# Two heads' score matmuls, and their products with values, issued as one run of four; rotary keys padded with zero rows

## Chip, cores and metric

The kernel runs on one core of one Trainium2 chip. The metric is the device time of one execution in microseconds (us); lower is better. TensorE (PE in the profile) multiplies matrices, with its weight loads shown as PEld; VectorE (DVE), ScalarE (ACT) and GpSimd (POOL) do the elementwise work, and SyncE (SP) issues the transfers.

## The reference

Four layers over 256 tokens of width 1024, batch 1, all in float32. What matters here are the attention parts:

- Layer 1 (AB): 8 heads of block attention with ALiBi ("moba", which at 256 tokens is plain causal attention) and 8 heads of forgetting attention ("fox"). Head width 64.
- Layer 2 (CD): 4 heads of differential attention (two score maps of width 64 each, values of width 128), and 8 heads of sliding-window attention ("swa") of width 64, where four query heads share one key head.
- Layer 3: latent attention ("MLA") with 8 heads; the score of a head is a product over 128 plain features plus a product over 64 rotary features, and the rotary keys are the same for all heads.
- Layer 4: stick-breaking attention. After layers 3 and 4 follow cross-attention to a memory and an MLP of width 4096.

```python
# one causal head of fox; moba, diff and swa have the same shape of work
s = einsum('bhqd,bhsd->bhqs', q, k) * scale + bias      # scores
p = softmax(where(causal, s, -inf))
o = einsum('bhqs,bhsd->bhqd', p, v)                     # product with values
# MLA: q = [q_nope (128) | q_rope (64)], k = [k_nope (128) | k_rope (64), shared by the heads]
```

## The kernel before

**Tiles.** The 256 queries and keys are two tiles of 128. Scores of a head are two matmuls in float32 into one PSUM bank: queries 0 to 127 against keys 0 to 127 (128 columns), and queries 128 to 255 against all 256 keys. Two heads of width 64 lie above each other in one transposed tile `qT[j]`, `kT[j]` (partitions 0 to 63 and 64 to 127), so a score matmul works on 64 of TensorE's 128 rows. In the profile these are the matmuls of form `64*128`. The product with values of moba, fox and swa has 64 columns of values as its weights, so it fills 64 of the 128 columns of the array (form `128*64`); two heads go to the two halves of the partitions of one bank. In MLA the rotary part of a score is again a matmul on 64 rows, added into the same bank as the plain part on 128 rows.

The trace has two matmul instructions for each of these float32 matmuls; they are called passes below. The large projections are not float32 matmuls: weights and activations are split into a high and a low part (type fp32r, form `psum<-r,r`), and three matmuls of one pass each stand for one product.

**Order.** Nothing is issued while the program is described. `Plan` records each instruction with its reads and writes, and `schedule` then simulates the five engines with a cost for each instruction, picks at each step the ready instruction with the longest chain behind it, gives out the slots of SBUF and PSUM, and so fixes an order for every engine. Each engine then runs its queue in that order. An attention part therefore does not run alone: between its matmuls the plan sets projection matmuls of the same or of the next stage.

**Names.** `scores` issues the two matmuls of one head; `soft` adds the bias, takes the maximum and the exponential on DVE and ACT; `normed` divides by the sums; `probs_T` transposes the probabilities with three TensorE transposes and a copy; `pv_feat` issues the two matmuls with the values; `gated` multiplies by the gate. In `layer_ab`, `layer_cd` and `mla` these are called head by head. `pairs_T` makes the transposed tiles, of the rotary keys `kpT` too. PSUM has 8 banks; at most 4 are given out for scores ("S").

Of the kernel before, what the change touches and what calls it, by code (L numbers as in the profile page):

```python
# [15 lines left out]
OP = mybir.AluOpType  # L16
AX = mybir.AxisListType.X
PSUM = bass.MemoryType.PSUM


# ======================================================================
# Recording: views of tiles that have no address yet
# ======================================================================
class Buf:
    """A tile to be: its slot is picked when its first instruction is scheduled."""

    def __init__(self, tag, np_, shape, dtype, name):
        self.tag, self.np_, self.dtype, self.name = tag, np_, dtype, name
        self.row = int(np.prod(shape))
        self.log = []          # (op, writes, p0, p1, mask)  # L30
        self.left = 0          # accesses not scheduled yet
        self.slot = None
        self.free_at = 0.0
        self.first = self.last = None


class Pool:
    """Slots for tiles. use[i]: the slots in use while instruction i runs, if from now on all
    instructions ran in the order of the program; as long as that fits, no deadlock is possible."""
# [114 lines left out]
# how long after the end of an instruction another engine may start  # L154
# [11 lines left out]
class Plan:  # L166
# [7 lines left out]
    # -- tiles  # L174
# [3 lines left out]
    def tag(self, name, pool, most=99, dtype=F32):  # L178
        """A kind of tile that lives in a pool, at most `most` at a time as long as others wait."""
        self.tags[name] = dict(pool=self.pools[pool], psum=pool == "psum", most=most, dtype=dtype, used=0)  # L180
# [11 lines left out]
    # -- instructions  # L192
    def op(self, forms, reads, writes, kind=""):
        """forms: {engine: (ns, call)}: the engines it may run on."""
        o = Op()
# [5 lines left out]
        for v, w in [(v, False) for v in reads] + [(v, True) for v in writes]:  # L201
            b = v.buf
# [12 lines left out]
            for e in b.log:  # L215
# [4 lines left out]
                # an older access that this write hides entirely need not be kept  # L220
# [11 lines left out]
    def either(self, *calls):  # L232
        """One instruction that any of several engines may run: (engine, method, args, kw) each."""
# [9 lines left out]
    # -- scheduling  # L243
    def schedule(self):
# [36 lines left out]
        def can(b):  # L281
            tg = self.tags[b.tag]
            p = tg["pool"]
            if b.first <= front:
                return bool(p.free)
            if not p.free or tg["used"] >= tg["most"]:
                return False
            return p.use[front:b.first].max() < p.bufs
# [11 lines left out]
        while n < len(ops):  # L300
# [23 lines left out]
            if e == "T":  # L324
                # the first by priority that the loading of its operand doesn't delay
# [10 lines left out]
            bad = next((b for b in news if not can(b)), None)  # L336
# [3 lines left out]
            # another engine that would be done with it sooner  # L340
# [71 lines left out]
    # -- emission  # L412
# [34 lines left out]
class _Eng:  # L447
    """Stands for an engine while the instructions are recorded."""
# [23 lines left out]
def make(plan, e, method, args, kw):  # L472
    """((cost, call), reads, writes, act tables) of one instruction."""
# [79 lines left out]
# pools of tiles: elements in a partition, tiles  # L553
POOLS = {"k4": (1024, 5), "k2": (512, 33), "r2": (512, 46), "k1": (256, 18), "k128": (128, 11), "k16": (16, 64),
         "kr": (128, 3), "psum": (512, 8)}
# kinds of tiles: pool, the most at a time
# [8 lines left out]
class Net:  # L565
# [26 lines left out]
    def copy(self, out, in_):  # L592
        """A copy, on ACT or DVE."""
# [6 lines left out]
    def wpiece(self, src, f, pat, fill="", parts=1, **kw):  # L600
        """One piece of a weight matrix, f elements in each partition, as hi and lo in parts of equal size."""
# [15 lines left out]
    def wtiles(self, w, k0, nk, c0, nc_, fill=""):  # L617
        """Weight rows of the chunks k0.., columns c0..: pieces of (hi, lo, first chunk, chunks)."""
# [23 lines left out]
    def new_T(self, n=NC8):  # L642
        """(hi, lo) of a transposed activation: a list over the chunks of [128, 256] views each."""
# [9 lines left out]
    def mm3(self, ps, st, mv, first, last):  # L653
        """ps += st.T mv, both operands as (hi, lo)."""
# [5 lines left out]
    def mm_tok(self, ps, xt, wh, wl, kc, kmap, t, first, last):  # L660
        """ps[tokens of t, :] += X W, the activations stationary."""
# [8 lines left out]
    def proj_tok(self, w, xt, c0, ncol, k0=0, nk=NC8, ps=None, first=True, last=True, x0=0, cls="acc", fill=""):  # L670
        """Both token tiles of X W[:, c0:c0+ncol] in PSUM."""
# [7 lines left out]
    def mm_feat(self, ps, first_in_bank, xt, wh, wl, c, last):  # L679
        """ps[features, 256 tokens] += W.T X.T for a chunk, the weights stationary."""  # L680
# [5 lines left out]
    def proj_feat(self, w, xt, c0, ncol, nk=NC8, cls=("acc", "acc"), fill=""):  # L686
        """W[:, c0:c0+ncol].T X.T: feature blocks of 128, two to a bank."""
# [20 lines left out]
    def rows_T(self, tag, n, parts):  # L708
        """Rows of 128 from DRAM, transposed into columns [128, n]."""
# [88 lines left out]
    def squares(self, x):  # L798
        """Sums of the squares of the rows, [128, tiles]; x[t] has two halves."""
# [14 lines left out]
    def setup_late(self):  # L814
# [22 lines left out]
        nc.vector.tensor_scalar(self.lam, self.lam, LAM_INIT, None, op0=OP.subtract)  # -lambda  # L837
# [31 lines left out]
    def new_x(self):  # L869
        """The residual's transpose: banks of two chunks, [128, 2, 256] each."""  # L870
        return [self.nc.tile([128, 2, 256], "x", "x") for _ in range(4)]

    def stats_sum(self, x):
        """x: [128, k, 256] views; the sums of squares over the features, [128 tokens, tiles] in PSUM."""
# [18 lines left out]
    def stats_x(self, ss=None):  # L893
        """rstd of the residual's rows: [128, tiles]."""
# [11 lines left out]
    def gained(self, x, g0):  # L906
        """x.T times the gain, as hi and lo."""
# [11 lines left out]
    def rstd_bc(self, r):  # L919
        """rstd along the free dimension, the same in every partition: [128, 256]."""  # L920
# [10 lines left out]
    def out_proj(self, w, yt, pieces):  # L931
        """x += (Y W).T for a [*, 1024] matrix; pieces: (first chunk, chunks, half of the columns)."""
# [25 lines left out]
    def qk_scale(self, qk, t):  # L958
        """qk: raw projections of token tile t; the per-head RMS norm without gain, in place."""
# [20 lines left out]
    def pairs_T(self, src, np_, g=None):  # L980
        """src[t] [128 tokens, np_*128]: its transpose, np_ views [128, 256], times a column."""
# [15 lines left out]
    def scores(self, qT, kT, rows):  # L997
        nc = self.nc
        s = self.ps("S")
        nc.tensor.matmul(s[:, 0:128], qT[rows, 0:128], kT[rows, 0:128], start=True, stop=True)  # L1000
        nc.tensor.matmul(s[:, 128:384], qT[rows, 128:256], kT[rows, 0:256], start=True, stop=True)
        return s

    def soft(self, s, b0, b1, sums=None, init=None, scale=None):
        """exp(s + bias - max), or of -scale * (s + bias),
        for the causal blocks (q0 | k0), (q1 | k0 k1); returns it and -max."""
# [12 lines left out]
    def probs_T(self, e):  # L1019
        """[128 q, (q0k0 | q1k0 | q1k1)] -> [128 k, (k0: q0 q1 | k1: q1)]."""  # L1020
# [13 lines left out]
    def gate(self, w, xt, c0, rbc):  # L1034
        """2 silu(g).T of 512 columns: 4 views [128, 256]."""
# [12 lines left out]
    def gated(self, yt, c, p, g, k):  # L1048
        """k * p * g into the chunk c of yt."""
# [4 lines left out]
    def values(self, w, xt, c0, n=512):  # L1054
        """A projection with the tokens on the partitions: a tile for each token tile."""
# [7 lines left out]
    def q_or_k(self, w, xt, c0, g=None):  # L1063
        """A projection of 512 columns, normalised per head and transposed: 4 views [128, 256], two heads each."""
# [7 lines left out]
    def normed(self, e, sums):  # L1072
        """The exponentials of soft over their sums."""
# [3 lines left out]

    def pv_feat(self, o, v, sl, pt):
        """o = (P V).T of a causal head; sl: its columns of v."""
# [5 lines left out]
    def forget(self, w, xt):  # L1085
        """FOX: c = cumsum(log f) in columns, -c in every partition along the keys (two tiles of 4 heads)."""
# [45 lines left out]
    def layer_ab(self):  # L1132
# [5 lines left out]
        for mix in range(2):  # L1138
# [7 lines left out]
            for j in range(4):  # L1146
                op = self.ps("O")[:, :256]
                for s in range(2):
# [541 lines left out]
```

## Time and profile before

| | |
|---|---|
| median of 3 runs | 987.67 us (986.16 to 987.92) |
| span of the profiled execution | 990.0 us |
| own time of the profiled execution beside its span | not given apart from it |
| mean granted TensorE clock | 0.994 of full speed |
| TensorE matmuls busy | 962.9 us, 97% |
| VectorE busy | 680.6 us, 69% |
| ScalarE busy | 571.4 us, 58% |
| transfers | 157.13 MB, mean 159 GB/s |

A busy time of matmuls contains the pipeline behind each one: a matmul of 256 columns is listed with some 280 ns although the next one starts much earlier. So the cost of a matmul is read from the distance between starts, not from its duration. All instructions carry line 533, the helper that emits them; forms, shapes and times tell them apart.

### The profile page before, as it was taken

What the parts mean: (1) busy time and instruction counts of PE and PEld (TensorE: products, weight loads), DVE (VectorE), ACT (ScalarE), POOL (GpSimd) and SP (SyncE); (2) the same over time, 40 slices, a digit from 0 to 9 for tenths busy, and PEclk for the clock granted to TensorE, in tenths of its full rate; (3) what the DMA queues carried; (4) which work ended last, traced back from release to release, by engine and by line L of the source; (5) the groups of instructions that cost most, each with busy time, mean ns of one, the idle gap of its engine ahead of it and who ended that gap; (6) DMA issues with size and microseconds to landing.
All of it is one profiled execution on the core that took longest, in us unless ns stands there. A gap on an engine that the chain in (4) does not pass through costs nothing.

```text
span 990.0 us, 18191 instructions
## 1 busy us (share of the span) xinstructions
PE 962.9 (97%) x6829; PEld 874.0 (88%) x6829; DVE 680.6 (69%) x1561; ACT 571.4 (58%) x1310; POOL 59.9 (6%) x94
## 2 busy tenths in 40 slices
PE   7899999999999999999999999899999999999997
PEld 5577778888979889999999999899899999999985
DVE  7687686787987854896655456765768777556654
ACT  5675585557676675775555445644666754344443
POOL 2124000040210200000000000000000000000000
PEclk9999999999999999999999999999999999999999
DMA  7978424654413523664565456635535554555641
GB/s 193 285 191 207 113 85 150 212 149 131 145 34 90 154 94 115 211 192 141 171 204 180 149 192 203 181 128 165 166 117 168 174 170 144 179 189 176 203 154 43
DMA packets 96678, 157.13 MB, mean 159 GB/s; under 512 B 9831, under 2 KB 28493, under 8 KB 96589
## 3 DMA queue, kind: packets, MB, share of 16 engines
q1 hardware_dynamic: 96236, 154.91, 50.8%
q8 instruction: 53, 0.87, 0.4%
q0 software_dynamic: 352, 1.06, 0.3%
q14 instruction: 37, 0.30, 0.1%
HBM read 154.89 MB, written 1.06 MB: 158 GB/s over the span
## 4 chain that ended last, share of the span: by engine, by line
PE 81%; DMA 9%; DVE 4%; ACT 2%; SPq 1%; issue 1%; POOL 1%; POOLq 0%; DVEq 0%; ACTq 0%
PE psum L533 81%; DMA k<-in_w_in_ab_dram 4%; DVE r L533 2%; DMA k<-in_mlp_w_out_dram 2%; DMA k<-in_sb_w_qkv_dram 2%; ACT r L533 2%; SPq L533 1%; DVE k L533 1%; ACT k L533 1%; POOL k L533 1%; DMA k<-in_mla_w_ukv_dram 0%; DMA k<-in_mla_w_uq_dram 0%; POOLq L1686 0%; DVEq L533 0%; ACTq L533 0%
## 5 line engine op out<-in xcount | busy, mean ns | idle before, releaser
L533 PE MATMUL psum<-r,r 128*128 128x256 f32 (+2 forms) x6018 | 891.9, 305 | 9.8 <-ACT r L533 9.1
L533 PEld LDWEIGHTS psum<-r,r 128*128 128x128 f32 x6018 | 795.6, 190 | 69.1 <-ACT r L533 13.3
L533 DVE TENSOR_TENSOR r<-k,r 128x512 fp32r<-128x512 f32 (+2 forms) x669 | 407.5, 648 | 149.2 <-ACT r L533 73.1
L533 ACT ACTIVATE r<-k 128x512 fp32r<-128x512 f32 (+2 forms) x568 | 310.7, 592 | 203.7 <-PE psum L533 84.2
L533 PE MATMUL psum<-k,k 128*128 128x128 f32 (+8 forms) x771 | 149.0, 316 | 10.3 <-DMA k<-in_x_dram 4.5
L533 ACT ACTIVATE k<-psum 128x256 f32<-128x256 f32 (+4 forms) x168 | 70.5, 451 | 124.0 <-PE psum L533 120.6
L533 PEld LDWEIGHTS psum<-k,k 128*128 128x128 f32 (+3 forms) x771 | 94.9, 166 | 38.3 <-issue 12.1
L533 POOL TENSOR_TENSOR k<-k,k 128x2 f32<-128x2 f32 (+3 forms) x42 | 49.8, 1200 | 884.9 <-DVE k L533 833.5
L533 ACT ACTIVATE k<-k 128x256 f32<-128x256 f32 (+4 forms) x147 | 71.7, 507 | 19.7 <-DVE k L533 15.4
L533 ACT ACTIVATE k<-k,k 128x256 f32<-128x256 f32 (+3 forms) x152 | 64.7, 450 | 19.1 <-DVE k L533 15.9
L533 DVE CAST r<-k 128x512 fp32r<-128x512 f32 (+2 forms) x101 | 40.0, 402 | 28.9 <-PE psum L533 12.2
L533 DVE TENSOR_TENSOR k<-k 128x256 f32<-128x256 f32 (+3 forms) x40 | 13.8, 344 | 40.9 <-ACT k L533 39.6
L533 DVE TENSOR_TENSOR k<-k,k 128x512 f32<-128x512 f32 (+5 forms) x86 | 40.3, 478 | 2.3 <-ACT k L533 1.3
L533 DVE TENSOR_TENSOR k<-psum,k 128x512 f32<-128x512 f32 (+2 forms) x53 | 33.4, 635 | 11.6 <-PE psum L533 11.3
L533 ACT ACTIVATE r<-k,k 128x256 fp32r<-128x256 f32 x64 | 29.7, 500 | 16.2 <-DVE k L533 15.1
L533 DVE SCALAR_TENSOR_TENSOR r<-k,k,r 128x256 fp32r<-128x256 f32 x72 | 34.3, 494 | 2.4 <-ACT r L533 1.5
L533 DVE TENSOR_TENSOR r<-psum,r 128x256 fp32r<-128x256 f32 (+1 forms) x52 | 24.0, 480 | 16.3 <-ACT r L533 14.7
L533 ACT ACTIVATE r<-psum 128x256 fp32r<-128x256 f32 (+1 forms) x49 | 20.7, 435 | 14.1 <-PE psum L533 13.8
L533 DVE TENSOR_SCALAR k<-k,k 128x128 f32<-128x128 f32 (+7 forms) x88 | 21.6, 274 | 5.2 <-POOL k L533 4.7
L533 ACT ACTIVATE k<-psum,k 128x512 f32<-128x512 f32 (+1 forms) x18 | 11.6, 650 | 13.2 <-PE psum L533 13.2
L533 DVE CUSTOM_DVE_ANT_0 k<-psum,k 128x256 f32<-128x256 f32 (+1 forms) x48 | 15.0, 353 | 4.8 <-PE psum L533 4.5
L533 DVE CUSTOM_DVE_ANT_0 k<-psum,k,k 128x256 f32<-128x256 f32 (+1 forms) x32 | 12.1, 414 | 8.3 <-PE psum L533 8.2
(39 smaller groups left out, 165.0 us busy)
## 6 DMA issues: line engine op xcount, KB each, us to landing
k<-in_mlp_w_in_dram SPq DMA_DIRECT2D x64, 512.0 KB, 4.6
k<-in_mlp_w_out_dram SPq DMA_DIRECT2D x64, 512.0 KB, 4.5
k<-in_w_in_ab_dram SPq DMA_DIRECT2D x32, 512.0 KB, 7.0
k<-in_w_in_cd_dram SPq DMA_DIRECT2D x26, 512.0 KB, 4.6
k<-in_sb_w_qkv_dram SPq DMA_DIRECT2D x24, 512.0 KB, 4.7
k<-in_xa_w_kv_dram SPq DMA_DIRECT2D x16, 512.0 KB, 5.5
k<-in_w_out_ab_dram SPq DMA_DIRECT2D x8, 512.0 KB, 3.7
k<-in_w_out_cd_dram SPq DMA_DIRECT2D x8, 512.0 KB, 4.5
```

The lines of the kernel that those rows point to most:

```text
L533: return getattr(eng, method)(*[real(a) for a in args], **{k: real(v) for k, v in kw.items()})
```

## The change

Three edits. First, `scores` takes both heads of a pair, and issues their four matmuls as one planned instruction, in the order: head 0 queries 0 to 127, head 1 queries 0 to 127, head 0 queries 128 to 255, head 1 queries 128 to 255. This holds for moba, fox and swa (pairs of heads) and for the two maps of a differential head. Second, `pv_pair` does the same for the products with values of moba, fox and swa: it is issued when the transposed probabilities of both heads are there. Third, in MLA the rotary keys are kept in two tiles of 128 rows, one with the keys in the upper 64 rows and zeros below, one the other way round, so that the rotary matmuls work on all 128 rows. The plan gets a new call `group` with a cost of its own, and `can` counts several new tiles of one instruction. The diff removes comments as well; these lines are left out here.

```diff
+    def group(self, *calls):
+
+        cost, load, gos, reads, writes = 190.0, None, [], [], []
+        for args, kw in calls:
+            (c, go, ld), r, w, _ = make(self, "T", "matmul", args, kw)
+            cost += 104 + 0.805 * args[2].size
+            load = ld if load is None else load
+            gos.append(go)
+            reads += r
+            writes += w
+
+        def go():
+            for g in gos:
+                g()
+
+        return self.op({"T": (cost, go, load)}, reads, writes, "group")
...
-        def can(b):
+        def can(b, before):
+
             tg = self.tags[b.tag]
             p = tg["pool"]
+            k = sum(self.tags[x.tag]["pool"] is p for x in before)
             if b.first <= front:
-                return bool(p.free)
-            if not p.free or tg["used"] >= tg["most"]:
+                return len(p.free) > k
+            if len(p.free) <= k or tg["used"] + sum(x.tag == b.tag for x in before) >= tg["most"]:
                 return False
-            return p.use[front:b.first].max() < p.bufs
+            return p.use[front:b.first].max() + k < p.bufs
...
-    def scores(self, qT, kT, rows):
-        nc = self.nc
-        s = self.ps("S")
-        nc.tensor.matmul(s[:, 0:128], qT[rows, 0:128], kT[rows, 0:128], start=True, stop=True)
-        nc.tensor.matmul(s[:, 128:384], qT[rows, 128:256], kT[rows, 0:256], start=True, stop=True)
-        return s
+    def scores(self, qT, kT):
+
+        res = [self.ps("S") for _ in range(2)]
+        calls = []
+        for q, k in ((slice(0, 128), slice(0, 128)), (slice(128, 256), slice(0, 256))):
+            for i, s in enumerate(res):
+                rows = slice(64 * i, 64 * i + 64)
+                o = s[:, 0:128] if q.start == 0 else s[:, 128:384]
+                calls.append(((o, qT[rows, q], kT[rows, k]), dict(start=True, stop=True)))
+        self.nc.group(*calls)
+        return res
...
+    def pv_pair(self, o, v, sls, pts):
+
+        calls = []
+        for k, (a, b), c in ((0, (0, 256), 0), (1, (256, 384), 128)):
+            for i, (sl, pt) in enumerate(zip(sls, pts)):
+                calls.append(((o[64 * i:64 * i + 64, c:256], v[k][:, sl], pt[:, a:b]),
+                              dict(start=k == 0, stop=k == 1, skip_group_check=True)))
+        self.nc.group(*calls)
...
             for j in range(4):
-                op = self.ps("O")[:, :256]
-                for s in range(2):
+                pts = []
+                for s, sc in enumerate(self.scores(qT[j], kT[j])):
                     h = 2 * j + s
-                    rows = slice(s * 64, (s + 1) * 64)
-                    sc = self.scores(qT[j], kT[j], rows)
...
                     self.normed(e, sums)
-                    self.pv_feat(op[rows], v, slice(h * 64, (h + 1) * 64), self.probs_T(e))
+                    pts.append(self.probs_T(e))
+                op = self.ps("O")[:, :256]
+                self.pv_pair(op, v, [slice(h * 64, (h + 1) * 64) for h in (2 * j, 2 * j + 1)], pts)
                 self.gated(yt, 4 * mix + j, op, g[j], 0.5)
...
-                for m in range(2):
-                    sc = self.scores(qT[h], kT[h], slice(m * 64, (m + 1) * 64))
+                for m, sc in enumerate(self.scores(qT[h], kT[h])):
...
-        kpT, = self.pairs_T([k.rearrange("p r d -> p (r d)") for k in kpd], 1)
+        p = self.ps("T")
+        for t in range(NT):
+            self.tr(p[:, t * 128:(t + 1) * 128], kpd[t].rearrange("p r d -> p (r d)"))
+
+        kpT = [self.t2([128, 256], "kpT") for _ in range(2)]
+        for s in range(2):
+            nc.gpsimd.memset(kpT[s][64 - 64 * s:128 - 64 * s], 0.0)
+            self.copy(kpT[s][64 * s:64 * s + 64], p[64 * s:64 * s + 64, :256])
...
-                nc.tensor.matmul(sc[:, 0:128], qpT[hh // 2][rows, 0:128], kpT[rows, 0:128], start=False, stop=True)
+                nc.tensor.matmul(sc[:, 0:128], qpT[hh // 2][:, 0:128], kpT[s][:, 0:128], start=False, stop=True)
                 nc.tensor.matmul(sc[:, 128:384], qn[h // 2][:, h % 2, 128:256], kn[h // 2][:, h % 2], start=True, stop=False)
-                nc.tensor.matmul(sc[:, 128:384], qpT[hh // 2][rows, 128:256], kpT[rows], start=False, stop=True)
+                nc.tensor.matmul(sc[:, 128:384], qpT[hh // 2][:, 128:256], kpT[s], start=False, stop=True)
```

In `layer_cd` the loop of swa is changed as the one of `layer_ab`.

## Rows read from the trace of the kernel before

**Rows 1.** The page: busy us, share of the span, instructions.

```profile
PE 962.9 (97%) x6829; PEld 874.0 (88%) x6829; DVE 680.6 (69%) x1561; ACT 571.4 (58%) x1310; POOL 59.9 (6%) x94
```

**Rows 2.** Who TensorE waited for after 85 us: us, times, longest.

```profile
PE psum L533 <- ACT r L533: 5.4, 6, 3.7
...
PE psum L533 <- DVE r L533: 0.2, 1, 0.2
```

**Rows 3.** The chain that ended last, in order of time: start, length, what.

```profile
78.17 5.36 DMA k<-in_w_in_ab_dram
...
85.24 182.24 PE psum L533 x1184
```

**Rows 4.** TensorE matmuls by form: rows*columns of the array, output, count, busy, mean ns.

```profile
L533 PE MATMUL psum<-k,k 64*128 64x256 f32 x80 | 19.8, 429 | 0.0
...
L533 PE MATMUL psum<-k,k 128*64 128x256 f32 x48 | 10.0, 404 | 0.0
```

**Rows 5.** Timeline of TensorE matmuls in fox: start, us from first start to last end.

```profile
119.87 0.40 PE L533 MATMUL psum<-r,r 128*128 128x512 f32 x1
120.20 0.49 PE L533 MATMUL psum<-k,k 64*128 64x128 f32 x4
120.62 0.38 PE L533 MATMUL psum<-r,r 128*128 128x256 f32 x1
120.84 0.40 PE L533 MATMUL psum<-r,r 128*128 128x256 f32 x2
...
121.75 0.70 PE L533 MATMUL psum<-k,k 64*128 64x256 f32 x4
122.38 0.51 PE L533 MATMUL psum<-r,r 128*128 128x256 f32 x2
```

**Rows 6.** Timeline, an unbroken run of projection matmuls in the first MLP.

```profile
604.81 5.46 PE L533 MATMUL psum<-r,r 128*128 128x256 f32 x45
```

**Rows 7.** Timeline, the scores of swa; a row is named by its first form.

```profile
273.27 0.93 PE L533 MATMUL psum<-k,k 64*128 64x128 f32 x8
274.13 0.62 PE L533 MATMUL psum<-r,r 128*128 128x256 f32 x3
...
277.01 0.92 PE L533 MATMUL psum<-k,k 64*128 64x128 f32 x4
277.86 0.97 PE L533 MATMUL psum<-r,r 128*128 128x256 f32 x6
278.76 0.92 PE L533 MATMUL psum<-k,k 64*128 64x128 f32 x4
```

**Rows 8.** Timeline, products with values in fox.

```profile
118.72 0.65 PE L533 MATMUL psum<-k,k 128*64 128x256 f32 x2
119.30 0.97 PE L533 MATMUL psum<-r,r 128*128 128x256 f32 x4
...
134.82 0.65 PE L533 MATMUL psum<-k,k 128*64 128x256 f32 x4
135.40 0.97 PE L533 MATMUL psum<-r,r 128*128 128x256 f32 x4
```

**Rows 9.** Timeline, the first and the last matmuls on half an array.

```profile
78.85 0.49 PE L533 MATMUL psum<-k,k 64*128 64x128 f32 x2
...
372.23 0.70 PE L533 MATMUL psum<-k,k 64*128 64x256 f32 x2
372.85 0.33 PE L533 MATMUL psum<-k,k 128*128 128x128 f32 x1
```

**Rows 10.** Stretch, length; busy PE, PEld, DVE, ACT, POOL; PEclk; DMA share; GB/s.

```profile
75.00:160.00 85.00, 83.80 (x531) 62.99 (x530) 63.90 (x197) 55.21 (x150) 9.64 (x8) 0.98 0.49 137
...
265.00:288.00 23.00, 21.93 (x147) 17.02 (x146) 20.99 (x82) 18.49 (x63) 6.36 (x8) 1.00 0.27 78
288.00:297.00 9.00, 9.00 (x63) 5.94 (x60) 6.08 (x19) 5.58 (x16) 0.00 (x0) 1.00 0.00 0
340.00:375.00 35.00, 35.00 (x226) 28.80 (x224) 22.07 (x72) 26.25 (x71) 0.86 (x1) 1.00 0.33 106
```

More of the change, by code (lines that the diff above doesn't have):

```diff
@@ L335, in schedule @@
             news = [b for b in o.bufs if b.slot is None]
-            bad = next((b for b in news if not can(b)), None)
+            bad = next((b for n_, b in enumerate(news) if not can(b, news[:n_])), None)
             if bad is not None:
@@ L1236, in layer_cd @@
         for j in range(4):
-            op = self.ps("O")[:, :256]
-            for s in range(2):
+            pts = []
+            for s, sc in enumerate(self.scores(qT[j], kT[j // 2])):
                 h = 2 * j + s
-                rows = slice(s * 64, (s + 1) * 64)
-                sc = self.scores(qT[j], kT[h // 4], rows)
                 bw = self.t2([128, 256], "bw")
@@ L1250, in layer_cd @@
                 self.normed(e, sums)
-                self.pv_feat(op[rows], v, slice(h // 4 * 64, (h // 4 + 1) * 64), self.probs_T(e))
+                pts.append(self.probs_T(e))
+            op = self.ps("O")[:, :256]
+            self.pv_pair(op, v, [slice(j // 2 * 64, (j // 2 + 1) * 64)] * 2, pts)
             self.gated(yt, 4 + j, op, g[j], 0.5)
@@ L1373, in mla @@
                 hh = 4 * g + h
-                rows = slice(s * 64, (s + 1) * 64)
                 sc = self.ps("S")
                 nc.tensor.matmul(sc[:, 0:128], qn[h // 2][:, h % 2, 0:128], kn[h // 2][:, h % 2, 0:128], start=True, stop=False)
-                nc.tensor.matmul(sc[:, 0:128], qpT[hh // 2][rows, 0:128], kpT[rows, 0:128], start=False, stop=True)
+                nc.tensor.matmul(sc[:, 0:128], qpT[hh // 2][:, 0:128], kpT[s][:, 0:128], start=False, stop=True)
                 nc.tensor.matmul(sc[:, 128:384], qn[h // 2][:, h % 2, 128:256], kn[h // 2][:, h % 2], start=True, stop=False)
-                nc.tensor.matmul(sc[:, 128:384], qpT[hh // 2][rows, 128:256], kpT[rows], start=False, stop=True)
+                nc.tensor.matmul(sc[:, 128:384], qpT[hh // 2][:, 128:256], kpT[s], start=False, stop=True)
                 sums = self.sm([128, NT], "msum")
```

## Prediction

> **What bounds the kernel now.** I read the page first: TensorE's matmuls are busy for 97% of the span, VectorE for 69%, ScalarE for 58% [rows 1]. Then TensorE's waits: after 85 us it waits for anyone for 8.5 us in all, in ten pieces and by five rows, of which the longest and the shortest are shown [rows 2]. Then the chain that ended last: up to 85 us it runs through weight transfers, after that through TensorE in long pieces, one of them from 85 to 267 us without a break [rows 3]. So from 85 us on a microsecond taken out of TensorE's queue is a microsecond of the kernel, as long as VectorE and ScalarE keep up. Because a busy TensorE need not be an efficient one, the last view is the timeline, from start to start. In an unbroken run of projection matmuls 256 columns take (5.46 - 0.28) / 44 = 0.118 us each [rows 6].
>
> **What a stay on half the array costs.** The matmuls on 64 rows or 64 columns stand in short runs between full-size ones; I call such a run a visit. Take one at 120.20 us [rows 5]. The 512-column matmul ahead of it started at 119.87; 512 columns at the granted 2.4 GHz stream for 0.21 us, so with 0.01 between neighbours the next could have started at 120.09: entering costs 0.10. Start of the visit to start of the next full matmul is 0.42. That next matmul then needs 0.22 to its successor instead of 0.118: another 0.10. So each visit costs 0.20 on top of its own length. That extra is 0.15 where a transpose follows; I use 0.20 throughout.
>
> The lengths, from the visit's start to the next full matmul: two heads, 128 columns: 0.42; two heads, 256 columns: 0.63 [rows 5]; one head, 256 columns: 0.62 [rows 9]; one head with both: 0.85; two heads with both, eight passes: 0.86 [rows 7]; values, 256 columns, one head 0.58 and two heads 0.58 [rows 8]. Taking 0.107 (256 float32 columns need two clocks each, 0.213 per pass; 128 need 0.107) off each of two passes, values with 128 columns come to 0.37, one head's scores with 128 columns to 0.41.
>
> Two things are to be seen. The second head is free when it stands beside the first: eight passes take as long as four. And the plan before already pairs heads often, but not always, and rarely joins the 128- and the 256-column part.
>
> **Counting.** There are 73 visits in the timeline, the first at 78.85, the last at 372.23 us [rows 9]. They hold 160 passes on 64 rows and 96 on 64 columns: 80 and 48 with 256 columns [rows 4], and as many with 128.
>
> - 47 on rows: 10 of one head with 128 columns (4.2 us), 8 with 256 (5.0), 9 of two heads with 128 (3.8), 9 with 256 (5.7), 6 of one head with both (5.1), 3 of two heads with nearly all (2.6), 2 mixed as long as a 256 (1.3): 27.7.
> - 26 on columns: 5 and 7 with 128 (4.4), 5 and 6 with 256 (6.4), 3 longer ones (0.8, 0.8, 1.5): 13.9.
> - 73 x 0.20 for entering and leaving: 14.6.
>
> Before: 56.2 us.
>
> After: 16 score groups (4 moba, 4 fox, 4 diff, 4 swa) at 0.86 + 0.20 = 17.0. Twelve value groups: two heads with 256 columns take 0.58, the two 128-column passes add 0.21 behind them, so 0.79 + 0.20, 11.9. MLA's rotary matmuls leave half-array mode: I let the step from 64 to 128 rows add nothing, since 128-row matmuls also stream a column per clock (256 in 0.118 us [rows 6]), so 8 heads x (2 x 0.107 + 2 x 0.213) = 5.1, and 0.2 for four steps of 0.005 to 0.01 a head. After: 34.2 us. **TensorE gets 22.0 us shorter**: some 10 in layer AB, 1.6 in diff, 5 in swa, 5 in MLA. Bounds: if each visit cost 0.15 instead of 0.20, the 45 visits that go away give 2.2 less; nothing in the rows gives more than 22.
>
> **What costs nothing, and why.** One more copy of 64 x 256 on ScalarE or VectorE and two fills on GpSimd, which is 6% busy [rows 1]. An instruction of ScalarE takes 26.25 / 71 = 0.37 us in MLA's stretch [rows 10]. The three are needed only when MLA's first scores start, after TensorE has projected queries, keys and values; without that cover they would cost three times that, 1.1 us, and nothing in them can gain time. The two tiles take one slot more of the 256-element pool. A score group needs two score banks at once out of four, which the plan enforces; a value group waits for both heads' probabilities, so its first head's product comes later and `gated` with it; behind it in TensorE's queue stand the projection matmuls.
>
> **Where the gain is not paid out.**
> - The first visits (78 to 85 us) lie where the chain runs through a weight transfer [rows 3]: 0.7 us lost.
> - In swa, 265 to 288 us, VectorE is busy for 20.99 of 23.00 us [rows 10]. It can follow TensorE by at most 2.0 us there; score visits shrink by 3.1 (7 visits, 7.4 us, to 4 x 1.06). 1.1 lost. At 288 to 297 VectorE has 2.9 us free for the other 2.0. In AB it has 21 of 85 free, for 10; in MLA ScalarE has 8.7 of 35 free, for 5 [rows 10].
> - All costs and readiness change, so the plan is drawn anew from about 78 us on, and the 8.5 us of waits will fall elsewhere. I add 1.0, an eighth of them, as an estimate; bounds -3 to +5.
>
> Sum against the profiled execution: 990.0 - 22.0 + 0.7 + 1.1 + 1.0 = 970.8. The median of the runs shown is 987.67, 2.3 below that span, so **968.5 us**, 1.9% faster.
>
> **A rule against it.** Eight passes of two heads took 0.86 us and four of one head 0.85 [rows 7], and 0.58 stands against 0.58 for values [rows 8]: passes of different halves ran together in whatever order they were queued. The Trainium skill, "TensorE: Matmul & The Clock Gate", Part 3, "The mechanism", says that matmuls start and end strictly in program order and only weight loads overtake. By that the sum would be 974.5, as worked out for the second rival; the rows here speak against it.
>
> **Rivals.**
> 1. *VectorE becomes the bound in the attention parts.* For: 91% busy in 265 to 288, and 63.90 of 85 in AB [rows 10], which becomes 85% if TensorE takes 75 us. Against: TensorE has projection matmuls to fill with, and the long chain piece covers all of fox. If swa's 5.1 and half of AB's 10 are lost: 968.5 - 1.1 (counted already) + 10.1 = 977.5.
> 2. *Passes overlap only at the seams of calls.* Each float32 call is two passes. If head 1's first pass must wait for head 0's second to start, a score group streams 0.107 + 0.107 + 0.213 + 0.213 + 0.213 = 0.85 instead of 0.64, a value group likewise: 28 x 0.21 = 6.0, giving 974.5. Against: rows 7 and 8.
> 3. *Slower: the value group blocks TensorE's queue.* In swa the heads follow each other by 1.75 us (277.01 to 278.76 [rows 7]), VectorE's pace. If the second head's probabilities are late by that each time and nothing is queued ahead, 12 groups cost 21 us: 989.5. It decides from 1.6 us a group (19.2 / 12); slower by over 0.2% from 1.8. Against: the plan places the group where it believes both are ready, and puts six projection matmuls between two visits even in swa.
> 4. *No change:* the pairs were together already, or another resource sets the pace. Against: 47 + 26 visits for what 28 can hold; the transfers use 0.49 of the DMA engines at most in these stretches [rows 10].
>
> **How the numbers follow.** Forecast 0.64 (own range 962 to 975: all 22.0 paid out and the waits 3 shorter gives 963, the waits 5 longer and 2.2 less gained 975), rival 1 0.20, rival 2 0.06, rival 3 0.06, no change 0.04. What a measurement of this kernel can tell from no change is about 0.2%, 2 us. Faster 0.64 + 0.20 + 0.06 = 0.90, within 0.2% 0.04, slower 0.06. The range reaches from 962 to 980, so that rival 1 is inside and rivals 3 and 4 are left out.
>
> **What would show it.** Passes of form 64*128 fall from 160 to 128, float32 passes on the full array rise by 32; 28 visits instead of 73, of 0.86 and 0.79. Right: TensorE's waits after 85 us stay near 8.5 and layer AB ends some 9 us earlier. Rival 1: waits for VectorE or ScalarE grow by several us between 75 and 300. Rival 2: score groups last 1.07. Rival 3: TensorE waits over a microsecond ahead of 128*64 runs. I am wrong if the new order opens waits outside the attention parts, which no row of before can show.

## The result, and the profile after

The changed kernel takes 970.56 us (median of 4 runs, 969.73 to 971.15); the kernel before, beside it, 987.13 (986.16 to 987.92). The ratio is 0.9825, interval 0.9809 to 0.9842: 16.6 us faster, where 19.2 were forecast, inside the range.

The span went from 990.0 to 968.0, by just the 22.0 us that the forecast takes out of TensorE. That is chance. The executions of the kernel before spread from 984.24 to 990.56 us over 29 runs. A time is some 1.7 us above its span (986.43 for 984.7), so the one profiled took some 991.7, more than any of them; a second profile of it has a span of 984.7 (first experiment below). Against that one the traces differ by 16.7, as the medians do. So the second trace of before stands for it from here on.

The page of the changed kernel, busy time by engine; it answers to [rows 1]:

```profile
span 968.0 us, 18191 instructions
...
PE 940.2 (97%) x6829; PEld 869.6 (90%) x6829; DVE 679.3 (70%) x1565; ACT 573.7 (59%) x1311; POOL 57.9 (6%) x96
```

TensorE has as many matmuls as before and is 22.7 us less busy than in the first profile, 19.4 less than in the second (959.6); all other engines are within 2.3 us of where they were. The forms, as in [rows 4]:

```profile
L552 PE MATMUL psum<-k,k 128*128 128x256 f32 x80 | 23.3, 382 | 0.1
...
L552 PE MATMUL psum<-k,k 64*128 64x256 f32 x64 | 10.6, 380 | 0.0
L552 PE MATMUL psum<-k,k 64*128 64x128 f32 x64 | 9.2, 320 | 1.3 <-DVE k L552 1.2
L552 PE MATMUL psum<-k,k 128*64 128x256 f32 x48 | 7.8, 402 | 0.0
L552 PE MATMUL psum<-k,k 128*64 128x128 f32 x48 | 4.7, 273 | 0.0
```

Passes on 64 rows fell from 160 to 128, as forecast. In the timeline they make 15 visits, those on 64 columns 11: 26, because two score groups (at 98.48) and two value groups (at 279.45) stand back to back, where 28 were forecast and 73 stood before.

Timeline of TensorE in fox, changed kernel: start, length, form of the first matmul of a run, count. It answers to [rows 5, 7, 8]:

```profile
123.45 0.93 PE L552 MATMUL psum<-k,k 64*128 64x128 f32 x8
124.30 0.98 PE L552 MATMUL psum<-r,r 128*128 128x256 f32 x6
...
127.65 0.87 PE L552 MATMUL psum<-k,k 128*64 128x256 f32 x8
128.45 0.50 PE L552 MATMUL psum<-r,r 128*128 128x512 f32 x1
```

A score group lasts 124.30 - 123.45 = 0.85 us (0.86 forecast), a value group 0.80 (0.79). Eleven of the sixteen score groups are like that; four before 104 us and one in swa are longer, by 1.3 us together (below, at the wait for the second bank). Who TensorE waited for after 85 us, answering to [rows 2]:

```profile
PE psum L552 <- ACT r L552: 3.5, 6, 1.0
PE psum L552 <- DVE k L552: 2.6, 3, 1.2
PE psum L552 <- ACT k L552: 0.8, 3, 0.3
PE psum L552 <- POOL k L552: 0.7, 1, 0.7
PE psum L552 <- DVE r L552: 0.3, 1, 0.3
```

7.9 us in all. The first profile of before has 8.5, its one long wait of 3.7 included; the second has 5.9, and one more of 1.1 at 84.51, just ahead of the window, so 7.0. So far everything is as forecast. A difference stands in the chain that ended last, of 78 to 125 us; it answers to [rows 3]:

```profile
85.82 7.39 DMA k<-in_w_in_ab_dram
...
93.89 1.29 DVE r L552 x2
...
98.18 1.14 ACT k L552 x2
...
99.33 1.28 ACT L452
...
101.63 1.28 ACT L452
...
103.81 21.24 PE psum L552 x140
```

Before, the chain was TensorE's from 85.24 us on (84.51 in the second profile). Now it goes on through another weight transfer and then through VectorE and ScalarE, until 103.81. Line 452 is `preload_act_table_set`, with which ScalarE loads another set of function tables. The same stretch by engine (stretch, length, busy PE, PEld, DVE, ACT, POOL, clock, DMA share, GB/s), first the second profile of the kernel before, then the changed one:

```profile
85.00:104.00 19.00, 18.98 (x113) 14.39 (x113) 11.78 (x46) 12.70 (x35) 0.00 (x0) 1.00 0.70 196
104.00:985.00 881.00, 867.47 (x6376) 800.93 (x6375) 603.98 (x1357) 507.19 (x1171) 33.49 (x33) 1.00 0.48 153
```

```profile
85.00:104.00 19.00, 17.42 (x119) 14.28 (x119) 17.47 (x64) 16.90 (x41) 1.36 (x3) 1.00 0.77 181
104.00:968.00 864.00, 849.99 (x6369) 798.30 (x6368) 598.32 (x1346) 503.93 (x1167) 32.52 (x35) 1.00 0.49 156
```

VectorE is busy for 17.47 of 19 us (11.78 before), ScalarE for 16.90 (12.70); four table loads of 1.28 us lie there where one did, which is nearly all of ScalarE's increase. At 104 us TensorE has done 461 matmuls: 329 of projections, 40 passes on 64 rows, 92 others. Before it had done 454: 334, 32, 88. So up to there almost nothing has been won, and the whole 881 - 864 = 17 us comes after it.

### The profile page after: what moved, and what is told of

It is laid out like the page before. It is cut to its first block, busy times and chain, and to the rows that moved or that the text cites. A ratio compares the mean times of both kernels' runs of the same rounds, so it can differ in the third digit from the quotient of the medians.

```text
span 968.0 us, 18191 instructions
## 1 busy us (share of the span) xinstructions
PE 940.2 (97%) x6829; PEld 869.6 (90%) x6829; DVE 679.3 (70%) x1565; ACT 573.7 (59%) x1311; POOL 57.9 (6%) x96
## 4 chain that ended last, share of the span: by engine, by line
PE 76%; DMA 12%; DVE 6%; ACT 3%; issue 1%; SPq 1%; POOL 1%; POOLq 0%; DVEq 0%; ACTq 0%
PE psum L552 76%; DMA k<-in_w_in_ab_dram 7%; DVE r L552 3%; DMA k<-in_mlp_w_out_dram 2%; DVE k L552 2%; ACT r L552 2%; ACT k L552 1%; DMA k<-in_sb_w_qkv_dram 1%; SPq L552 1%; POOL k L552 1%; DMA k<-in_xa_w_kv_dram 1%; DMA k<-in_mlp_w_in_dram 1%; DMA k<-in_xa_w_o_dram 0%; DMA k<-in_xa_w_q_dram 0%; DMA k<-in_mla_w_uq_dram 0%
## 5 line engine op out<-in xcount | busy, mean ns | idle before, releaser
L552 PE MATMUL psum<-r,r 128*128 128x256 f32 (+1 forms) x6018 | 882.8, 304 | 9.6 <-ACT r L552 7.9
L552 ACT ACTIVATE r<-k 128x512 fp32r<-128x512 f32 (+3 forms) x567 | 311.2, 592 | 206.2 <-PE psum L552 100.4
L552 PE MATMUL psum<-k,k 128*128 128x128 f32 (+8 forms) x771 | 132.9, 307 | 11.2 <-DVE k L552 5.4
L552 ACT ACTIVATE k<-psum 128x256 f32<-128x256 f32 (+5 forms) x171 | 71.5, 453 | 111.2 <-PE psum L552 109.1
L552 PEld LDWEIGHTS psum<-k,k 128*128 128x128 f32 (+3 forms) x771 | 92.0, 166 | 27.3 <-DVE k L552 7.4
L552 ACT ACTIVATE k<-k,k 128x128 f32<-128x128 f32 (+3 forms) x143 | 60.7, 448 | 11.0 <-DVE k L552 7.1
L552 DVE TENSOR_TENSOR k<-k,k 128x512 f32<-128x512 f32 (+4 forms) x86 | 40.2, 480 | 1.6 <-ACT k L552 0.8
L552 DVE TENSOR_TENSOR k<-k 128x256 f32<-128x256 f32 (+3 forms) x38 | 12.9, 341 | 38.4 <-ACT k L552 38.2
L552 DVE TENSOR_SCALAR k<-k,k 128x8 f32<-128x8 f32 (+7 forms) x97 | 24.5, 281 | 5.0 <-POOL k L552 4.5
L552 ACT ACTIVATION_READ_ACCUMULATOR k<-k,k 128x1 f32 x80 | 15.2, 190 | 0.0
```

Source lines behind the costliest of these rows:

```text
L552: return getattr(eng, method)(*[real(a) for a in args], **{k: real(v) for k, v in kw.items()})
```

## The experiments

The differences in us are differences of ratios to the kernel before, times 987; for the changed kernel the ratio is the mean of 0.9825 and 0.9815 (the first result and the second look just below), 0.982. The intervals make such a difference uncertain by about 2 us.

**A second look at both.** The kernel before and the changed one, not edited.

> The kernel before, unchanged, for a second profile. Theory (the profiled execution of before was a slow one: its 3.7 us wait at 639 us in the first stick-breaking projection, and the two half-rate clock stretches at 86.7 and 639.7 us that the new kernel's trace lacks, belong to that execution): span near 985.5, no wait above 2 us after 85 us. Rival (they belong to the kernel, and the change removed them): span 990 again, with the wait and the low clock in the same places.

986.43 us, span 984.7. Its waits after 85 us:

```profile
PE psum L533 <- ACT r L533: 4.0, 7, 1.9
PE psum L533 <- POOL k L533: 1.3, 1, 1.3
PE psum L533 <- DVE k L533: 0.4, 1, 0.4
PE psum L533 <- DVE r L533: 0.2, 1, 0.2
```

The longest is 1.9, against 3.7 in the first profile [rows 2]. Both stand ahead of the same matmul (at 635.67 and 639.23), and in the six profiles with the changed kernel's order a wait of 0.2 to 1.7 us stands there too: the wait belongs to the kernels, its length to the execution. In the first profile the granted clock was at half, 1.2 GHz, for 3.4 us from 86.7 and again from 639.7, each time soon after TensorE had waited (1.20 us up to 85.24, 3.69 up to 639.23). Around the second place TensorE was busy for 4.77 of 8 us and the clock was 0.79 in the mean. In the second profile, which has both waits too, the clock never fell between 33.8 and 982.7 us. From the first profile (columns as in the rows by engine above):

```profile
86.70:90.10 3.40, 3.40 (x13) 2.46 (x12) 3.21 (x12) 3.31 (x10) 0.00 (x0) 0.50 0.99 372
636.00:644.00 8.00, 4.77 (x27) 4.77 (x28) 5.72 (x11) 5.85 (x13) 0.00 (x0) 0.79 0.20 70
```

From 275 to 375 fp32r matmuls (the projections' form) the second profile's lead over the first goes from 0.6 to 1.75 us, and at the end it is 5.3. So single profiles of one kernel differ by as much as the terms that are looked for.

> The changed kernel itself, timed beside the next three. Both theories: ratio to before 0.981 to 0.985, as when it was timed first.

969.67 us (968.59 to 971.40), ratio 0.9815 [0.9800, 0.9830]: the same as the first result.

**One part alone.** Each kernel is the changed one with the other two parts undone. The score groups alone:

```diff
-                self.pv_pair(op, v, [...], pts)
+                    self.pv_feat(op[64 * s:64 * s + 64], v, ..., self.probs_T(e))
...
-                nc.tensor.matmul(sc[:, 0:128], qpT[hh // 2][:, 0:128], kpT[s][:, 0:128], ...)
+                nc.tensor.matmul(sc[:, 0:128], qpT[hh // 2][rows, 0:128], kpT[rows, 0:128], ...)
```

> Only the score groups; products with values head by head, rotary matmuls on 64 rows as before. Theory (the gain is the length of the visits to half an array): 33 score visits, 26.8 us, become 16 of 1.06, 17.0 us: 9.8 us less TensorE, of which 7 to 10 reach the end. Rival (a group holds two score banks and starves the other work): less than 4, with more waits of TensorE between 75 and 300 us.

987.16 us (985.37 to 993.69), ratio 1.0014 [0.9996, 1.0032]: nothing gained, a miss. The profile is of the slowest execution, 993.69. The timeline of TensorE (its weight loads next to it) shows a step that the forecast doesn't have:

```profile
78.30 0.48 PE L552 MATMUL psum<-k,k 64*128 64x128 f32 x2
79.71 1.18 PE L552 MATMUL psum<-k,k 64*128 64x128 f32 x7 [0.93 <-ACT k L552]
```

```profile
79.71 0.52 PEld L552 LDWEIGHTS psum<-k,k 64*128 64x128 f32 x6 [1.12 <-ACT k L552]
```

The group starts, does two passes, and stands until ScalarE has read the old scores out of the second bank. 7 of the 16 score groups are longer than 0.86, by 0.13 to 1.4 us each, 4.9 us in all; where the profile names who ended such a stand, it is ScalarE or VectorE. In `schedule` the time from which an instruction's new tiles are free is that of the first free slot of the pool, for every new tile; a group that takes two is started when one is free.

The value groups alone:

```diff
-        for s, sc in enumerate(self.scores(qT[j], kT[j])):
+        for s, sc in enumerate(self.scores_each(qT[j], kT[j])):
```

> Only the groups of products with values; scores head by head, rotary matmuls on 64 rows. Theory: 26 visits, 19.1 us, become 12 of 0.99, 11.9 us: 5 to 7 us faster. Rival (the group waits in TensorE's queue for the second head's probabilities): no faster than 2 us, with waits of TensorE ahead of the 128*64 runs.

990.87 us (986.79 to 997.69), ratio 1.0050 [1.0025, 1.0075]: slower, another miss. `scores_each` issues the scores head by head, and the rotary edit is undone too. Here the granted clock is a rival to any cause in the instructions. Six of the twelve executions took 986.79 to 989.15 us at a mean clock of 0.989 to 0.993, the other six 992.59 to 997.69 at 0.981 to 0.984; the 29 of the kernel before have 0.992 to 0.997. The profile is of the fastest. In it the clock is at half for 3.4 us from 87.2 and from 333.0, again soon after waits of TensorE (1.8 us up to 86.23, 1.9 up to 332.59). So part of the 4.9 us is probably the clock's; how much, and what this plan would give at the usual clock, no run shows.

The rotary keys alone:

> Only the rotary keys padded to 128 rows. Theory: 14 visits, 10.3 us, become 5.3 us of full-array matmuls: 4 to 5 us faster, all of it between 325 and 380 us. Rival (the half-array matmuls there were hidden behind ScalarE's softmax): within 1 us of before.

983.64 us, ratio 0.9966 [0.9952, 0.9980], 3.4 us faster, a little under what was expected. Its trace has the gain where it was expected: against the second trace of before it is 0.3 us behind when 1400 fp32r matmuls are done (314 us), ahead of MLA's rotary matmuls, and 4.5 us ahead when 1800 are (387 us). The parts alone come to +1.4, +4.9 and -3.4 us, and together to -17 or -18: they don't add up, and each of these kernels has a plan of its own. What a new plan alone does had to be measured.

**A new plan with the same instructions.** In the changed kernel a group's planned cost is 10 ns higher; in the kernel before that of each float32 matmul is.

```diff
-        cost, load, gos, reads, writes = 190.0, None, [], [], []
+        cost, load, gos, reads, writes = 200.0, None, [], [], []
```

> The changed kernel with the planned cost of a group raised by 10 ns, under 1%: the same instructions in another order. Theory (a plan drawn anew scatters): the same visits, 17.0 and 11.9 us, yet a time that may differ by 2 to 5 us from the changed kernel, with TensorE's waits in other places. Rival (the order matters little): within 1 us.

973.57 us, ratio 0.9857 [0.9842, 0.9871]: 3.7 us slower than the changed kernel, with the same groups (in 28 visits, since no two stand back to back). Its waits after 85 us are 9.7 us (ACT r 4.8, DVE r 1.8, DVE k 1.6, ACT k 1.3, POOL k 0.2) against 7.9.

```diff
-        cost = 2 * max(2 * N / 2.4, load) + 2
+        cost = 2 * max(2 * N / 2.4, load) + 12
```

> The kernel before, with the planned cost of a float32 matmul raised by 10 ns: the same instructions in another order. Theory (a plan drawn anew scatters, as the 3.9 us between the two plans of the changed kernel show): 2 to 5 us from the kernel before, in either direction, with visits of the same kinds. Rival (the plan of before is one of many alike): within 1 us.

995.49 us, ratio 1.0082 [1.0062, 1.0103]: 8.1 us slower than the kernel before, more than expected, with 77 visits for 73. In these two cases a plan drawn anew cost 4 and 8 us without any other change. That is as much as each part was to bring, so the times of one part alone can't price a part.

**The wait for the second bank.** The k-th new tile of a pool counts as free from the k-th free slot on:

```diff
-            late = max([min(self.tags[b.tag]["pool"].free)[0] for b in news], default=0.0)
+            late, seen_ = 0.0, {}
+            for b in news:
+                p = self.tags[b.tag]["pool"]
+                late = max(late, sorted(p.free)[seen_.get(p, 0)][0])
+                seen_[p] = seen_.get(p, 0) + 1
```

> The changed kernel, but the plan counts the time at which the second new score bank of a group comes free, where it took the first free bank's time for both. Theory (a group starts while its second bank is still being read, and TensorE then stands still inside the group): the 1.3 us of waits inside score groups between 78 and 100 us go away; 0.5 to 2 us faster than the changed kernel, give or take 3 us for a plan drawn anew. Rival (those waits are late operands, not late banks): the groups still hold gaps of over 0.2 us.

972.66 us, ratio 0.9836 [0.9817, 0.9855]. Every score group now runs through, the early ones too (timeline, first group; then the first group of the changed kernel, which lasts 1.46, up to a transpose at 80.71 that this view counts with it):

```profile
81.91 0.93 PE L556 MATMUL psum<-k,k 64*128 64x128 f32 x8
82.77 0.96 PE L556 MATMUL psum<-r,r 128*128 128x256 f32 x4
```

```profile
79.25 1.78 PE L552 MATMUL psum<-k,k 64*128 64x128 f32 x9
80.79 0.71 PE L552 MATMUL psum<-r,r 128*128 128x512 f32 x2
```

The wait is real, and the edit takes it away. But TensorE's waits after 85 us come to 10.0 us instead of 7.9, for ACT r 6.9 of it, and the kernel isn't faster (1.6 us slower, within the uncertainty of 2). What was a wait inside the groups became waits elsewhere in the new plan.

**The order inside a group.** Head 0's two matmuls, then head 1's two, for scores and values alike:

```diff
-        for q, k in ((slice(0, 128), slice(0, 128)), (slice(128, 256), slice(0, 256))):
-            for i, s in enumerate(res):
+        for i, s in enumerate(res):
+            for q, k in ((slice(0, 128), slice(0, 128)), (slice(128, 256), slice(0, 256))):
```

> The changed kernel with another order inside each group: both matmuls of head 0, then both of head 1. Theory (two halves of the array run side by side in whatever order they stand in the queue): groups of 0.86 and 0.79 as before, within 3 us of the changed kernel. Rival (passes overlap only where two neighbours in the queue belong to different halves): a score group takes 1.29, a value group 1.32, 16 x 0.43 + 12 x 0.53, together 13 us slower than the changed kernel.

969.23 us, ratio 0.9809 [0.9790, 0.9828]: no difference from the changed kernel. Timeline in fox:

```profile
124.81 0.93 PE L552 MATMUL psum<-k,k 64*128 64x128 f32 x8
125.67 0.98 PE L552 MATMUL psum<-r,r 128*128 128x256 f32 x6
...
129.03 0.88 PE L552 MATMUL psum<-k,k 128*64 128x256 f32 x8
129.83 0.84 PE L552 MATMUL psum<-r,r 128*128 128x512 f32 x3
```

0.86 and 0.80 again. The two heads run beside each other however they are queued.

**Parts taken back with every queue held.** Three kernels keep the order of all queues; only what TensorE streams is different, so the plan plays no part. An added matmul costs nothing in the plan, which keeps it from changing. First, each score group is split by a full-array matmul of one column between its 128- and its 256-column matmuls; its column is not used.

```diff
+            if q.start == 0:
+                calls.append(((res[0][:, 384:385], self.ident, self.onec), dict(start=True, stop=True)))
```

> The changed kernel with every engine's queue in the same order, and one thing added: inside each of the 16 score groups a float32 matmul of one column on the full array, between the 128- and the 256-column calls, so that a visit becomes two. Its output goes to an unused column. Theory (a visit costs entering and leaving): a group of 0.86 becomes 0.42 + 0.63, plus 0.20 for the second visit, plus some 0.2 for the added matmul with its two loads: 0.5 to 0.6 each, 8 to 10 us slower than the changed kernel. Rival (other engines set the pace in these parts): under 2 us.

975.59 us, ratio 0.9889 [0.9871, 0.9907], 6.8 us slower than the changed kernel; a little less than expected. A group:

```profile
126.98 1.44 PE L552 MATMUL psum<-k,k 64*128 64x128 f32 x10
128.34 0.98 PE L552 MATMUL psum<-r,r 128*128 128x256 f32 x6
```

1.36 instead of 0.86: 16 x 0.50 = 8.0 us, of which 6.8 arrive. Second, the rotary matmuls read only the 64 rows with keys in them:

```diff
-                nc.tensor.matmul(sc[:, 0:128], qpT[hh // 2][:, 0:128], kpT[s][:, 0:128], ...)
+                nc.tensor.matmul(sc[:, 0:128], qpT[hh // 2][64 * s:64 * s + 64, 0:128], kpT[s][64 * s:64 * s + 64, 0:128], ...)
...
```

> The changed kernel with every engine's queue in the same order, but the rotary matmuls of MLA read only the 64 rows that hold keys (the zero rows are there and unread). Theory: 14 to 16 visits, 10.3 to 11.5 us, where 5.3 us stood: 5 to 6 us slower than the changed kernel. Rival (ScalarE's softmax sets the pace in MLA): under 1 us. Beside e4, where the plan was drawn anew, it shows how far one plan tells the price of an edit.

973.36 us, ratio 0.9874 [0.9854, 0.9894]: 5.3 us slower, as expected. Reading half the rows costs more than reading all of them, since each such matmul is a visit:

```profile
350.71 0.48 PE L552 MATMUL psum<-k,k 64*128 64x128 f32 x2
351.13 0.39 PE L552 MATMUL psum<-r,r 128*128 128x256 f32 x1
```

Third, each value group does head 0, then one column on the full array, added to a part of the bank that isn't used, then head 1:

```diff
...
+            if i == 1:
...
+                calls.append(((bank, self.ident, self.onec), dict(start=False, stop=False, ...)))
```

> The changed kernel with every engine's queue in the same order; in each of the 12 value groups head 0's two matmuls, then a float32 matmul of one column on the full array into an unused column, then head 1's two. Theory (the second head is free only beside the first): a group of 0.79 becomes two of 0.79, plus 0.20 for the second visit and 0.2 for the added matmul: 12 to 15 us slower than the changed kernel. Rival (the group waits for the second head's probabilities anyway, so the first head's time is hidden): under 4 us.

982.36 us, ratio 0.9951 [0.9933, 0.9969]: 12.9 us slower, as expected.

```profile
133.44 1.97 PE L552 MATMUL psum<-k,k 128*64 128x256 f32 x10
135.34 0.85 PE L552 MATMUL psum<-r,r 128*128 128x512 f32 x3
```

1.90 instead of 0.80, 12 x 1.10 = 13.2. Twelve groups of TensorE's queue made longer are paid nearly in full: where the value groups stand, from 118 us on, its queue is the bound in the changed kernel as before.

## Why the prediction was right, and where it was off

**The price of a visit: right.** Leaving the full array and coming back was put at 0.20 us beside the stay. Read as in the forecast, 18 visits of the changed kernel that stand between projection matmuls cost 0.09 us on entering and 0.11 on leaving. The runs with the queues held fit it. The 15 visits of the rotary matmuls on half the rows last 7.9 us, with 15 x 0.20 so 10.9, where by the forecast 5.3 stood: 5.6 more, and 5.3 were measured. A rotary matmul with 128 columns lasts 0.42 (forecast 0.41). The other two add a matmul of one column as well: 0.50 for a split and 1.10 for two visits in place of one, each some 0.1 less than the steps of their expectations (0.59 and 1.19), so these two don't give the price by itself. Of the 8.0 and 13.2 us that TensorE's queue gets longer, 6.8 and 12.9 are seen in the time. The Trainium skill, "TensorEngine Tiling (Array Packing)", "Key Properties", says that a change of tiling mode drains TensorE; the trace agrees, with 0.09 and 0.11 us at the two ends of a visit.

**The second head is free: right.** 0.85 and 0.80 a group, in either order. The rule weighed in the forecast (the Trainium skill, "TensorE: Matmul & The Clock Gate", Part 3, "The mechanism": starts and ends strictly in program order) is not borne out here. Queued head by head, head 1's first pass would by it start no sooner than head 0's last, 0.107 + 0.107 + 0.213 = 0.43 us later, and the group would take 1.29 in place of 0.86; 0.86 was measured, with the first passes of the two heads 13 ns apart. Rival 2 falls with it.

**The count and the rotary keys: right.** 26 visits for 28, and with the queues held 5.3 us for the rotary keys, where 5 were forecast in MLA.

**No value group blocks the queue (rival 3).** Nothing waits ahead of the 128*64 runs: both rows of that form have 0.0 idle. Rival 4 falls by the time itself.

**What is not paid out: mis-sized.** The forecast loses 2.8 of 22.0 us; between the second trace of before (984.7) and that of the changed kernel (968.0) 5.3 are lost. Where they go is seen at equal places of TensorE's work. One is the first transpose after the output projection of AB, with 830 fp32r matmuls ahead of it in both traces (timeline, second profile of before, then the changed kernel):

```profile
204.05 0.27 PE L533 MATMUL psum<-k,k 128*128 128x128 f32 x1
```

```profile
197.29 0.27 PE L552 MATMUL psum<-k,k 128*128 128x128 f32 x1
```

So AB brings 6.8 us here, and 5.3 to 5.6 in three other profiles of the same plan (second look, head by head, rotary on half), where the forecast had some 10 less 0.7. The sign "layer AB ends some 9 us earlier" was missed by 2 to 4 us; only against the first trace of before, with its 3.4 us at half the clock in AB, is it 8.5. By the same reading, in the changed kernel, its second look and head by head, diff brings 1.7 (1.6 forecast), swa 4.2 to 5.0 (5 less 1.1) and MLA 5.4 to 5.5 (5), and behind MLA 0.8 to 2.3 are lost again. The parts with a VectorE term came out as well as forecast or better; the misses are AB and what lies behind MLA.

The step that failed is the first of its list: "The first visits (78 to 85 us) lie where the chain runs through a weight transfer [rows 3]: 0.7 us lost". The border of 85 us was read from the trace of before and kept for the changed kernel. But 85 us was where the chain passed to TensorE in the old plan; in the new one it passes at 103.81. What that costs, by the forecast's own prices: on 64 rows 27.7 + 47 x 0.20 = 37.1 us for 160 passes before, 0.232 each, and 17.0 for 128 after, 0.133 each. The 40 passes done by 104 us should have saved 40 x 0.099 = 4.0. The lead at 104 us is 8 passes (8 x 0.232 = 1.9) less five projection matmuls (5 x 0.118 = 0.6), so 1.3 us. Hence 2.7 lost and not 0.7; with the three other profiles of this plan (323 to 325 projection matmuls and 40 passes by 104 us) 3.2 to 3.4. So in the first of these profiles the term is 2.0 too small, where AB falls 2.5 short (9.3 less 6.8), and in the others 2.5 to 2.7, where AB falls 3.7 to 4.0 short.

What fills this stretch is less sure. It looks like rival 1 in a place where the forecast did not seek it: VectorE and ScalarE are at 17.47 and 16.90 of 19 us while the weights still come in, since the plan brings moba's heads forward there (64 VectorE instructions for 46). But the sign of rival 1, waits for VectorE or ScalarE several us longer between 75 and 300 us, did not come: they are 3.4 us, against 2.1 in the second trace of before. And a busy VectorE alone costs little elsewhere: in swa it is busy for 12.74 of 13 us, and swa brought what was forecast.

```profile
263.00:276.00 13.00, 12.04 (x99) 9.49 (x97) 12.74 (x64) 11.20 (x47) 3.23 (x6) 1.00 0.14 40
```

A second term was put at nothing: the forecast counts one more copy on ScalarE or VectorE, but the new plan also has four more table loads on ScalarE, 5.1 us, and two of them stand in the chain above (99.33 and 101.63):

```profile
L433 ACT ACT_TABLE_LOAD x5 | 6.4, 1283 | 0.1
```

```profile
L452 ACT ACT_TABLE_LOAD x9 | 11.5, 1283 | 0.2
```

Neither is shown to be the cause. In the run with the second bank's time the chain passes to TensorE at 97.25 already, with no table load in it between 75 and 97 us, and yet AB brings 5.8, no more than here. No run removes the transfer, the elementwise work or the table loads there, so the cause of the 2 to 3 us stays open.

**The plan drawn anew: too narrow.** +1.0 with bounds of -3 to +5 was taken; two plans with the same instructions as their parents came out 3.7 and 8.1 us slower. That the time still fell inside the range is in part luck: a miss of 8 us would have been possible. Much of what a plan costs lies where no edit reaches: when 1800 fp32r matmuls are done, near the end of MLA, the run with the raised group cost is 18.0 us ahead of the second trace of before and the run with the second bank's time 16.4, like the changed kernel's plan (17.0 to 18.9); at the end they are 13.3 and 13.1 ahead, and the changed kernel's plan 15.0 to 16.6. The group that starts with one of its two banks still taken was not foreseen either: inside its groups the changed kernel loses 1.3 us by it. Its waits for DVE k and ACT k after 85 us are 3.4 us, against 0.4 in the second trace of before, or 1.5 with the one at 84.51; all lie ahead of 283 us and outside the groups. Since mending the start of the groups moves the waits and gains nothing, it can't be counted as lost time.

**What stays open.** Why the score groups alone gain nothing and the value groups alone lose 4.9 us. The waits for the second bank (4.9 us in the first), the lower clock (in the second) and a new plan (4 to 8 us) may each be large enough, but no run divides them. No version beat the changed kernel: head by head, at 0.9809, is equal to it within the intervals.

## What to carry to other kernels

On a queue that bounds the kernel, count how often TensorE goes to half the array and back (here 0.20 us each time) and pair what fits side by side; a zero-padded full array can be cheaper than a half (5.3 us over MLA's 8 heads). Don't carry the place where an engine becomes the bound over from the trace of before: here the chain passed to TensorE at 97 to 105 us in the profiles of three new plans (with the score groups whole), instead of 85. In a kernel whose order comes from a planner, price an edit with all queues held, since a plan drawn anew moved the time by as much as the edit, and compare traces at equal places of the work (after so many matmuls) before a loss is put down to a place.

## What the runs showed of the hardware

The paired passes of two heads overlap even when all of one head's matmuls are queued ahead of the other's (0.86 and 0.80 us either way). A single column on the full array between two half-array runs costs 0.50 us where it splits a score group. A visit to half the array costs 0.09 us on entering and 0.11 on leaving. A load of ScalarE's function tables takes 1.28 us. Executions of the kernel before differ by some 6 us (984.24 to 990.56). In one profile of it the granted clock was at half for 3.4 us, twice, each time soon after TensorE had waited; in the other, with waits at the same matmuls, it was not; around the first of these places the other one's lead grew from 0.6 to 1.75 us.
